# Mixer stage of two fused transformer blocks on one core: conv taps in turns over two channel blocks, four taps instead of eight as matrix products, a reordered projection, and work moved to ScalarE

## The chip, the cores and the metric

One core of one Trainium2 chip runs the whole program. The metric is the device time of one execution in microseconds; the median of several executions is compared.

## What is computed

The reference is a `first_block` and then two layers of a `second_block`, on 256 tokens of width 1024, all in fp32. Only one stage of the first block is touched, the mixer between its two feed-forward layers:

```python
z = _rmsnorm(h, mix_norm[i]) @ w_in[i]
conv_a, conv_gt, q, k, v, r, g_lr = jnp.split(z, SPLIT_POINTS, axis=-1)
y_conv = _conv_module(conv_a, conv_gt, conv_w[i], conv_b[i], conv_ln_g[i], conv_ln_b[i])
y_gla = _gla(q, k, v, r, g_lr, gate_w_up[i], gate_b[i], gla_norm[i])
h = h + jnp.concatenate([y_conv, y_gla], axis=-1) @ w_out[i]
```

`_conv_module` takes `a * sigmoid(b)` (512 channels), runs a causal depthwise convolution of 31 taps over the tokens, adds a bias, and applies a layer norm over the channels and silu. `_gla` is a gated linear attention (here: GLA) of 4 heads over chunks of 64 tokens: `log_sigmoid` of a low-rank gate is summed up within a chunk, its exponentials scale q and k, the scores inside a chunk take one of two products on either side of the diagonal, a state is carried from chunk to chunk, and the result is normalised by head and multiplied by `silu(r)`.

## The kernel before

Every large matrix product is made of three: operands are split into a high part (a cast to fp32r, ScalarE, L208) and a low part (the rest, a subtraction on VectorE, L209), and high x high, low x high and high x low are added up in PSUM. The weights come in one fixed order (`stream_keys`, from `main_keys`, L83) in pieces of 1 MB (SP's DMA queue, L182, three buffers); each piece is split in two halves of 128x1024, tiles `wh` and `wl`, of which eight can be live. `Stream.release` (L222) gives a half back after its last use and at once issues the split of the next one (`pump`, L186). Two shapes of product are used: `chunk` (L667, 24 matmuls of 512 columns for one token tile, L505 to L507) and `chunkT` (L685, 96 matmuls of 256 columns, transposed output, L707).

The order of the instructions of an engine is fixed when the program is built: each takes a priority from its place in the program, and `ahead(-n)` puts it n places further back. The weight splits are put back by 200 (`BEHIND`), the convolution taps by 500 (`CONV_BEHIND`). Side work is written as generators (`spawn`) that are resumed when a count of modelled TensorE time (`tick`) has gone on far enough; `conv_q` is a list of taps from which `tick` takes three for each such microsecond (`CONV_RATE`). At run time an engine executes its instructions in that fixed order and waits where an operand isn't ready.

The mixer (`mixer`, L1062) projects in this order: v of token tile 0 (`val`), the first two channel blocks of the convolution input for both token tiles (`ab`, key `("mi", 0)`), v of tile 1, the low-rank gate `glr`, q and k (`("mi", 2)`), the other two channel blocks (`("mi", 1)`), and r for both tiles (`("mi", 4)`). `glu_T` (L1068) turns the first two blocks so that the channels lie on partitions. The convolution is then, for each of four blocks of 128 channels, a tile `cacc` of 128x256 to which 31 shifted and scaled copies of `glu` are added: the first 23 on VectorE (one tensor_scalar at L832, 22 scalar_tensor_tensor at L839, all reading and writing the same `cacc`), the last 8 on TensorE as products with diagonal matrices (`conv_diag` makes these on ScalarE, L853; `conv_pe`, L856, runs the products at L863 and adds them at L867). `conv_end` (L870) turns `cacc` back to token rows (`cy`), takes the statistics (L876), normalises (`cn`, L884), turns again (`cyT`), applies silu (`cs`, L891) and splits (`cHL`).

GLA runs beside it: `gla_gates` (L899: `z`, `az`, `mz`, `cum`, `epn`, `ee`), `gla_scores` (L943: scaled q and k, `sc`), `gla_state` (L983: `kv`, `S`), `gla_out` (L1015: `o`, the reciprocal root on POOL, `y`, `yT`, `yHL`). The output projection accumulates its attention half (rows of `yHL`) first, for both token tiles, and then its convolution half (rows of `cHL`): 

```python
self.down(0, units(2, 0, self.yg), True, False)
while self.conv_q:
    self.conv_q.pop(0)()
ce = [self.spawn(self.conv_end(t)) for t in range(NT)]
self.down(1, units(2, 1, self.yg), True, False)
for t in range(NT):
    self.need(ce[t])
    self.down(t, units(0, t, self.yc), False, True)
    fin(t)
```

## Time and profile before

| what | us |
|---|---|
| median of three runs | 1488.61 |
| lowest, highest | 1487.82, 1488.87 |
| the profiled execution, its own time | 1489.93 |
| its span | 1488.1 |

The profile is of one execution. A timeline row gives the start, the listed duration, engine, source line, operation, tiles (written <- read), shapes and how many instructions are merged; in brackets the engine's idle time before it and what ended it. Listed durations of neighbouring instructions of one engine overlap a little, so the cost of one in a row of equals is the distance of their starts. A row of the view by stretches gives, for a stretch of time, its length, then the busy time of TensorE's matmuls (PE), weight loads (PEld), VectorE (DVE), ScalarE (ACT) and GpSimd (POOL), the clock granted to TensorE as a share of 2.4 GHz, and the DMA's share and rate.

### The profile page before, as it was taken

To read this page: it belongs to the slowest core of one execution; us is meant where nothing else is said; L and a number is where in the kernel's file an instruction comes from. 1 tells how busy PE (TensorE), PEld (TensorE's weight loads), DVE (VectorE), ACT (ScalarE), POOL (GpSimd) and SP (SyncE) were. 2 spreads that over 40 slices of the span, in tenths; PEclk is the share of its full clock that TensorE was granted. 3 is DMA by queue.
4 is the path that set the end of the run, shared out by engine and by line. 5 is a ranking of instruction groups with operands and counts; after the bars stand their busy time and mean duration, and the time that the engine had idled before them with its cause. 6 is when DMAs were issued, how large, how long until landed. Compare 5 with 4: busy or idle time off the path is not lost.

```text
span 1488.1 us, 23272 instructions
## 1 busy us (share of the span) xinstructions
PE 1459.3 (98%) x9256; PEld 1300.7 (87%) x9256; DVE 1086.9 (73%) x1693; ACT 782.2 (53%) x1238; POOL 55.3 (4%) x60
## 2 busy tenths in 40 slices
PE   8999999999999999999998999999999999999998
PEld 6999989779999879999777899998899988889997
DVE  6876569978875688765678798866988658685554
ACT  6545566265444585444576554446544455554442
POOL 1000000100000000000122100000000000000000
PEclk9999999999999999999999999999999999999999
DMA  8887545138776449786445389863888836376550
GB/s 321 324 310 270 194 147 182 68 131 321 296 298 230 149 156 351 284 317 210 153 144 198 115 331 351 338 236 126 318 345 338 305 140 236 105 296 226 210 201 29
DMA packets 52332, 346.06 MB, mean 233 GB/s; under 512 B 5912, under 2 KB 8704, under 8 KB 11776
## 3 DMA queue, kind: packets, MB, share of 16 engines
q1 hardware_dynamic: 52224, 344.58, 62.4%
q8 instruction: 72, 1.18, 0.3%
q14 instruction: 36, 0.29, 0.1%
HBM read 343.47 MB, written 1.09 MB: 232 GB/s over the span
## 4 chain that ended last, share of the span: by engine, by line
PE 81%; DVE 9%; ACT 4%; issue 2%; DMA 2%; POOL 2%; SPq 0%; POOLq 0%; DVEq 0%; ACTq 0%
PE gu L707 40%; PE acc L506 9%; PE acc L507 9%; PE acc L505 9%; DVE wl L209 4%; PE gu L506 2%; PE gu L507 2%; PE gu L505 2%; DMA raw<-wpack 2%; ACT wh L208 1%; PE xT L586 1%; DVE cacc L839 1%; POOL rn L519 1%; ACT s L1290 1%; PE cv L863 1%
## 5 line engine op out<-in xcount | busy, mean ns | idle before, releaser
L209 DVE TENSOR_TENSOR wl<-raw,wh 128x1024 fp32r<-128x1024 f32 x490 | 588.4, 1221 | 245.1 <-ACT wh L208 241.8
L208 ACT CAST wh<-raw 128x1024 fp32r<-128x1024 f32 x490 | 502.5, 1051 | 389.3 <-DMA raw<-wpack 150.8
L707 PE MATMUL gu<-xh,wh 128*128 128x256 f32 x1728 | 484.1, 280 | 1.1 <-DVE g L751 0.7
L707 PE MATMUL gu<-xl,wh 128*128 128x256 f32 x1728 | 482.5, 279 | 0.0
L707 PE MATMUL gu<-xh,wl 128*128 128x256 f32 x1728 | 482.0, 279 | 0.0
L707 PEld LDWEIGHTS gu<-xh,wh 128*128 128x128 f32 x1728 | 324.7, 188 | 4.4 <-DVE g L751 1.1
L707 PEld LDWEIGHTS gu<-xl,wh 128*128 128x128 f32 x1728 | 324.8, 188 | 2.5
L707 PEld LDWEIGHTS gu<-xh,wl 128*128 128x128 f32 x1728 | 324.8, 188 | 0.0
L506 PE MATMUL acc<-wh,g 128*128 128x512 f32 x528 | 206.7, 391 | 0.0
L507 PE MATMUL acc<-wl,g 128*128 128x512 f32 x528 | 206.0, 390 | 0.0
L505 PE MATMUL acc<-wh,g 128*128 128x512 f32 x528 | 205.8, 391 | 0.0
L462 DVE SCALAR_TENSOR_TENSOR raw<-raw,cact 128x1024 f32<-128x1024 f32 x144 | 171.6, 1218 | 10.0 <-DMA raw<-wpack 10.0
L507 PEld LDWEIGHTS acc<-wl,g 128*128 128x128 f32 x528 | 99.1, 188 | 21.0
L506 PEld LDWEIGHTS acc<-wh,g 128*128 128x128 f32 x528 | 99.1, 188 | 19.8 <-DVE g L514 1.4
L505 PEld LDWEIGHTS acc<-wh,g 128*128 128x128 f32 x528 | 99.1, 188 | 19.2
L749 ACT ACTIVATE s<-gu 128x256 f32<-128x256 f32 x108 | 40.4, 382 | 81.7 <-PE gu L707 81.7
L505 PE MATMUL gu<-wh,xh 128*128 128x512 f32 x192 | 75.7, 395 | 1.8 <-ACT wh L208 1.5
L507 PE MATMUL gu<-wl,xh 128*128 128x512 f32 x192 | 75.1, 393 | 1.5 <-DVE wl L209 1.5
L506 PE MATMUL gu<-wh,xl 128*128 128x512 f32 x192 | 75.3, 393 | 0.5 <-DVE xl L514 0.5
L751 DVE TENSOR_TENSOR g<-gu,s 128x256 f32<-128x256 f32 x108 | 44.4, 420 | 31.4 <-ACT s L749 31.3
L519 POOL TENSOR_TENSOR rn<-nv,neghalf 128x1 f32<-128x1 f32 (+1 forms) x22 | 20.1, 912 | 1238.5 <-DVE nv L533 1020.9
L513 ACT CAST g<-g 128x256 fp32r<-128x256 f32 x108 | 43.1, 405 | 36.1 <-DVE g L751 35.1
(308 smaller groups left out, 1622.1 us busy)
## 6 DMA issues: line engine op xcount, KB each, us to landing
raw<-wpack SPq DMA_DIRECT2D x316, 1024.0 KB, 4.9
gate<-grow SPq DMA_DIRECT2D x6, 512.0 KB, 4.4
row<-rows SPq DMA_DIRECT2D x5, 512.0 KB, 4.8
bias<-fd SPq DMA_DIRECT2D x16, 128.0 KB, 3.9
raw<-wpack SPq DMA_DIRECT2D x2, 512.0 KB, 7.5
out<-h SPq DMA_DIRECT2D x4, 256.0 KB, 2.2
h<-x SPq DMA_DIRECT2D x2, 256.0 KB
h<-x SPq DMA_DIRECT2D x1, 512.0 KB
```

Of the source, the lines that this page charges most:

```text
L208: self.last = k.after(nc.scalar.copy(out=h, in_=raw[:, u, :]))
L209: k.after(nc.vector.tensor_sub(out=l, in0=raw[:, u, :], in1=h.bitcast(F32)))
L462: self.after(nc.vector.scalar_tensor_tensor(out=raw[:, u, :], in0=raw[:, u, :], scalar=1.0, in1=self.cact, op0=ALU.mult, op1=ALU.mult, acc ...
L505: nc.tensor.matmul(out, lhsT=xh, rhs=wh, start=first, stop=False)
L506: nc.tensor.matmul(out, lhsT=xl, rhs=wh, start=False, stop=False)
L507: nc.tensor.matmul(out, lhsT=xh, rhs=wl, start=False, stop=last)
L513: self.nc.scalar.copy(out=dst[0], in_=src),
L519: self.nc.gpsimd.tensor_tensor(out=r, in0=v, in1=self.neghalf[:, :n], op=ALU.pow)
L586: self.last_T = nc.tensor.transpose(ps[:, i, :], xn[hf][:, i * P : (i + 1) * P], self.ident)
L707: nc.tensor.matmul(out, lhsT=ww, rhs=xx, start=first and n == 0, stop=last and n == 2, skip_group_check=True)
L749: nc.scalar.activation(s, b[:, 0, :], AF.Silu)
L751: nc.vector.tensor_mul(out=y, in0=b[:, 1, :], in1=s)
```

## The change

The number of taps done as products falls from 8 to 4. A block's accumulator now starts as the product plus the bias, written by ScalarE, and the remaining 27 taps follow on VectorE, queued alternately for the two blocks of a pair. The pair of blocks 0 and 1 gets its products inside `glu_T`, the pair 2 and 3 right after `glr`; the projection `("mi", 1)` and its weights move ahead of `glr`, q and k. Four pieces of GLA move from VectorE to ScalarE: the minimum in the gates becomes a Relu of the negated sum, four of the eight masked copies of the scores become eight plain copies of 64x64 blocks, the first state is copied there, and the squares of the output are summed there instead of by a reduction.

```diff
--- before.py
+++ after.py
@@ -48,7 +48,7 @@
 
 CONV_RATE = 3.0
 
-CONV_PE = 8
+CONV_PE = 4
 ADA_END = 12.0
 ADA_START = 4
 ADA_STOP = 7
@@ -82,7 +82,7 @@
 
 def main_keys():
     b1 = ffn_keys("f1")
-    b1 += [("mi", c, i) for c in (3, 0, 2, 1, 4) for i in range(2)]
+    b1 += [("mi", c, i) for c in (3, 0, 1, 2, 4) for i in range(2)]
     b1 += [("mo", i) for i in (2, 3, 0, 1)]
     b1 += ffn_keys("f2")
     b1 += [("pp", 0)] + [("pg", i) for i in range(4)]
@@ -824,36 +824,8 @@
         nc.sync.dma_start(out=self.glan, in_=self.row(R_GLA, 512))
         self.diags = self.spawn(self.conv_diag())
 
-    def conv_taps(self, b):
-
-        nc = self.nc
-        cw = COLS["conv_w"][0] + 31 * b
-        acc, glu = self.cacc[:, b, :], self.glu[b]
-        nc.vector.tensor_scalar(
-            out=acc, in0=glu[:, 0:S], scalar1=self.cols[:, cw : cw + 1], scalar2=self.col("conv_b", b),
-            op0=ALU.mult, op1=ALU.add,
-        )
-        for j in range(1, 31 - CONV_PE):
-            def tap(j=j):
-                with self.ahead(-CONV_BEHIND):
-                    nc.vector.scalar_tensor_tensor(
-                        out=acc, in0=glu[:, j : j + S], scalar=self.cols[:, cw + j : cw + j + 1], in1=acc,
-                        op0=ALU.mult, op1=ALU.add,
-                    )
-            self.conv_q.append(tap)
-
-    def conv_diag(self):
-
-        self.diag = {}
-        for b in range(4):
-            self.diag[b] = self.t("row", "diag", [P, 8, P])
-            for n in range(CONV_PE):
-                yield 5.0
-                at = COLS["conv_w"][0] + 31 * b + 31 - CONV_PE + n
-                i = self.nc.scalar.mul(self.diag[b][:, n, :], self.ident, self.cols[:, at : at + 1])
-                self.after(i, self.ws.last)
-
-    def conv_pe(self, bs):
+    def conv(self, bs):
+
 
         nc = self.nc
         ps = self.pst("cv", [P, 2, S])
@@ -864,8 +836,30 @@
                     ps[:, i, :], lhsT=self.diag[b][:, n, :], rhs=self.glu[b][:, j : j + S],
                     start=n == 0, stop=n == CONV_PE - 1,
                 )
-            nc.vector.tensor_add(out=self.cacc[:, b, :], in0=self.cacc[:, b, :], in1=ps[:, i, :])
+            nc.scalar.activation(self.cacc[:, b, :], ps[:, i, :], AF.Identity, bias=self.col("conv_b", b))
         self.tick(0.43 * CONV_PE * len(bs))
+        for j in range(31 - CONV_PE):
+            for b in bs:
+                def tap(j=j, b=b):
+                    at = COLS["conv_w"][0] + 31 * b + j
+                    acc = self.cacc[:, b, :]
+                    with self.ahead(-CONV_BEHIND):
+                        nc.vector.scalar_tensor_tensor(
+                            out=acc, in0=self.glu[b][:, j : j + S], scalar=self.cols[:, at : at + 1], in1=acc,
+                            op0=ALU.mult, op1=ALU.add,
+                        )
+                self.conv_q.append(tap)
+
+    def conv_diag(self):
+
+        self.diag = {}
+        for b in range(4):
+            self.diag[b] = self.t("row", "diag", [P, CONV_PE, P])
+            for n in range(CONV_PE):
+                yield 5.0
+                at = COLS["conv_w"][0] + 31 * b + 31 - CONV_PE + n
+                i = self.nc.scalar.mul(self.diag[b][:, n, :], self.ident, self.cols[:, at : at + 1])
+                self.after(i, self.ws.last)
 
     def conv_end(self, t):
         nc = self.nc
@@ -905,20 +899,23 @@
         nc.gpsimd.memset(rmask.rearrange("p (c t) -> p c t", t=64)[:, :, 0:1], 0.0)
         for hp in range(2):
             nc.tensor.matmul(pz[:, hp, :], lhsT=self.gup[:, hp * P : (hp + 1) * P], rhs=zt, start=True, stop=True)
+
         az = self.t("g2", "az", [P, 2, S])
         mz = self.t("g2", "mz", [P, 2, S])
+        nb = self.tiny("ngb", 2, 1)
+        nc.vector.tensor_scalar_mul(nb, self.col("gate_b"), -1.0)
         for hp in range(2):
-            b = self.col("gate_b", hp)
-            nc.scalar.activation(az[:, hp, :], pz[:, hp, :], AF.Abs, bias=b)
-            nc.vector.tensor_scalar(out=mz[:, hp, :], in0=pz[:, hp, :], scalar1=b, scalar2=0.0, op0=ALU.add, op1=ALU.min)
+            nc.scalar.activation(az[:, hp, :], pz[:, hp, :], AF.Abs, bias=self.col("gate_b", hp))
+            nc.scalar.activation(mz[:, hp, :], pz[:, hp, :], AF.Relu, scale=-1.0, bias=nb[:, hp : hp + 1])
         nc.scalar.activation(az, az, AF.Exp, scale=-1.0)
         nc.scalar.activation(az, az, AF.Ln, bias=1.0)
         yield 4.0
-        nc.vector.tensor_sub(out=mz, in0=mz, in1=az)
+        nc.vector.tensor_add(out=mz, in0=mz, in1=az)
         cum = self.t("g2", "cum", [P, 2, S])
         for hp in range(2):
             nc.vector.tensor_tensor_scan(cum[:, hp, :], rmask, mz[:, hp, :], 0.0, op0=ALU.mult, op1=ALU.add)
-        T = 1.0 / 16.0
+
+        T = -1.0 / 16.0
         be = self.tiny("be", 8, 1)
         nc.vector.tensor_scalar_mul(
             be.rearrange("p (a b) -> p a b", a=2), cum.rearrange("p a (c t) -> p a c t", t=64)[:, :, :, 63], T
@@ -975,9 +972,11 @@
                         nc.tensor.matmul(
                             ps[:, lu, hp, :], lhsT=kk[rows, hp, tok], rhs=qq[rows, hp, tok], start=True, stop=True
                         )
-                for lu, at in enumerate((K_LOW, K_UP)):
-                    m = self.kc[:, at : at + P].bitcast(I32)[:, None, :].to_broadcast([P, 2, P])
-                    nc.vector.copy_predicated(self.sc[t][:, e, :, :], m, ps[:, lu, :, :])
+                for c in range(2):
+                    cc = slice(64 * c, 64 * c + 64)
+                    nc.scalar.copy(out=self.sc[t][cc, e, :, cc], in_=ps[cc, 0, :, cc])
+                m = self.kc[:, K_UP : K_UP + P].bitcast(I32)[:, None, :].to_broadcast([P, 2, P])
+                nc.vector.copy_predicated(self.sc[t][:, e, :, :], m, ps[:, 1, :, :])
             yield 0.6
 
     def gla_state(self, c):
@@ -996,7 +995,7 @@
             self.states = self.t("b4", "S", [P, 4, 2, P])
         s = self.states[:, c]
         if c == 0:
-            nc.vector.tensor_copy(s, ps)
+            nc.scalar.copy(out=s, in_=ps)
         else:
             for hp in range(2):
                 nc.vector.scalar_tensor_tensor(
@@ -1039,9 +1038,9 @@
                         ps[64 * cc : 64 * cc + 64, hp, :], lhsT=self.qp[rows, hp, 64 * c : 64 * c + 64],
                         rhs=self.st[c][rows, hp, :], start=False, stop=True, skip_group_check=True,
                     )
-            sq = self.t("ev", "sq", [P, 2, P])
-            nc.scalar.activation(sq, ps, AF.Square)
-            nc.vector.tensor_reduce(out=ss.rearrange("p (a b) -> p a b", b=2)[:, :, e], in_=sq, op=ALU.add, axis=AX.X)
+            for hp in range(2):
+                h = 2 * hp + e
+                nc.scalar.activation(self.junk()[:, 0:P], ps[:, hp, :], AF.Square, accum_out=ss[:, h : h + 1])
         nc.vector.tensor_scalar(out=ss, in0=ss, scalar1=1.0 / P, scalar2=EPS, op0=ALU.mult, op1=ALU.add)
         r = self.rsqrt(ss, 4, f"g{t}")
         yield 3.5
@@ -1072,9 +1071,9 @@
             if t == NT - 1:
                 for i in range(2):
                     nc.scalar.copy(out=self.glu[i][:, 30 : 30 + S], in_=pt[i])
-                yield 0.5
-                for i in range(2):
-                    self.conv_taps(i)
+                self.conv_rate = CONV_RATE
+                yield 2.0
+                self.conv((0, 1))
 
         def ab(t):
             b = self.psg("ab")
@@ -1092,12 +1091,18 @@
                 self.vt = self.t("b4", "v", [P, NT, 512])
             nc.scalar.copy(out=self.vt[:, t, :], in_=ps)
 
+        self.need(self.diags)
         val(0)
         pt = [self.pst("gluT", [P, S]) for _ in range(2)]
         ab(0)
         ab(1)
-        self.conv_rate = CONV_RATE
         val(1)
+        banks = [self.psa("ab", i, [P, 2, S]) for i in range(2)]
+        self.chunkT(("mi", 1), banks)
+        for i, b in enumerate(banks):
+            sg = self.t("ev", "sig")
+            nc.scalar.activation(sg, b[:, 1, :], AF.Sigmoid)
+            nc.vector.tensor_mul(out=self.glu[2 + i][:, 30 : 30 + S], in0=b[:, 0, :], in1=sg)
 
         pz = self.psg("glr", [P, S])
         for k in range(KT):
@@ -1105,6 +1110,7 @@
                 pz, (self.wglr[0][:, k, :], self.wglr[1][:, k, :]), (self.xh[:, :, k, :], self.xl[:, :, k, :]),
                 k == 0, k == KT - 1,
             )
+        self.conv((2, 3))
         zt = self.t("ev", "glrT", [16, S])
         nc.scalar.copy(out=zt, in_=pz[0:16, :])
 
@@ -1116,15 +1122,6 @@
         banks = [self.psg("qk", [P, 2, S]) for _ in range(2)]
         self.chunkT(("mi", 2), banks)
         scores = self.spawn(self.gla_scores(banks, gates))
-        banks = [self.psa("ab", i, [P, 2, S]) for i in range(2)]
-        self.chunkT(("mi", 1), banks)
-        for i, b in enumerate(banks):
-            sg = self.t("ev", "sig")
-            nc.scalar.activation(sg, b[:, 1, :], AF.Sigmoid)
-            nc.vector.tensor_mul(out=self.glu[2 + i][:, 30 : 30 + S], in0=b[:, 0, :], in1=sg)
-            self.conv_taps(2 + i)
-        self.need(self.diags)
-        self.conv_pe((0, 1))
         states = self.spawn(self.gla_states(scores))
         outs = []
         for t in range(NT):
@@ -1135,7 +1132,6 @@
             nc.scalar.activation(self.rt[:, t, :], ps, AF.Silu)
             nc.gpsimd.tensor_mul(out=self.rt[:, t, :], in0=self.rt[:, t, :], in1=self.glan)
             outs.append(self.spawn(self.gla_out(t, [scores, states])))
-        self.conv_pe((2, 3))
         for o in outs:
             self.need(o)
         self.new_acc()
```

## Rows read from the trace of the kernel before

**Rows 1.** The page: busy time and share of the span of each engine.

```profile
PE 1459.3 (98%) x9256; PEld 1300.7 (87%) x9256; DVE 1086.9 (73%) x1693; ACT 782.2 (53%) x1238; POOL 55.3 (4%) x60
```

**Rows 2.** View by stretches; columns as told above.

```profile
223.70:299.80 76.10, 74.30 (x485) 63.37 (x484) 71.56 (x159) 31.93 (x49) 6.55 (x4) 1.00 0.32 120
```

**Rows 3.** Timeline of VectorE, the end of the convolution.

```profile
294.20 4.64 DVE L839 SCALAR_TENSOR_TENSOR cacc<-glu,cols,cacc 128x256 f32<-128x256 f32 x9
298.95 0.42 DVE L867 TENSOR_TENSOR cacc<-cacc,cv 128x256 f32<-128x256 f32 x1
299.79 1.30 DVE L876 BATCH_NORM_STATS2 cst<-cy 128x6 f32<-128x512 f32 x2 [0.42 <-PE cy L874]
303.47 2.35 DVE L209 TENSOR_TENSOR wl<-raw,wh 128x1024 fp32r<-128x1024 f32 x2
```

**Rows 4.** Timeline of TensorE, a product group and the output projection.

```profile
278.96 3.61 PE L863 MATMUL cv<-glu,diag 128*128 128x256 f32 x16
282.41 0.61 PE L1028 MATMUL o<-v,sc 128*128 128x128 f32 x4
...
301.64 0.39 PE L507 MATMUL acc<-wl,yHL 128*128 128x512 f32 x1
301.87 0.40 PE L505 MATMUL acc<-wh,yHL 128*128 128x512 f32 x1
...
304.57 0.39 PE L507 MATMUL acc<-wl,yHL 128*128 128x512 f32 x1
306.06 0.73 PE L505 MATMUL acc<-wh,cHL 128*128 128x512 f32 x2 [1.10 <-ACT cHL L513]
```

**Rows 5.** Timeline of VectorE, where the taps begin.

```profile
223.75 0.73 DVE L832 TENSOR_SCALAR cacc<-glu,cols 128x256 f32<-128x256 f32 x2
...
224.79 2.35 DVE L209 TENSOR_TENSOR wl<-raw,wh 128x1024 fp32r<-128x1024 f32 x2
227.06 3.25 DVE L839 SCALAR_TENSOR_TENSOR cacc<-glu,cols,cacc 128x256 f32<-128x256 f32 x8
230.25 0.48 DVE L913 TENSOR_SCALAR mz<-z,cols 128x256 f32<-128x256 f32 x1
```

**Rows 6.** Groups of VectorE from 223.7 to 299.7 us: busy, mean ns | idle before.

```profile
L839 DVE SCALAR_TENSOR_TENSOR cacc<-glu,cols,cacc 128x256 f32<-128x256 f32 x88 | 38.2, 488 | 0.3
L209 DVE TENSOR_TENSOR wl<-raw,wh 128x1024 fp32r<-128x1024 f32 x15 | 17.9, 1217 | 0.7 <-ACT wh L208 0.7
L980 DVE COPY_PREDICATED sc<-kc,sc 128x256 f32<-128x256 int32 x8 | 3.0, 431 | 0.0
...
L1044 DVE TENSOR_REDUCE gs<-sq 128x2 f32<-128x256 f32 x4 | 1.6, 412 | 1.0 <-ACT sq L1043 1.0
```

**Rows 7.** Timeline of ScalarE, the copies of glu.

```profile
222.48 0.64 ACT L1074 COPY glu<-gluT 128x256 f32<-128x256 f32 x2
```

**Rows 8.** Chain of waits, one chunkT product: start, length.

```profile
122.24 11.20 PE gu L707 x96
```

**Rows 9.** Timeline of VectorE, weight splits and taps.

```profile
278.09 3.48 DVE L209 TENSOR_TENSOR wl<-raw,wh 128x1024 fp32r<-128x1024 f32 x3
281.50 3.07 DVE L839 SCALAR_TENSOR_TENSOR cacc<-glu,cols,cacc 128x256 f32<-128x256 f32 x5
```

**Rows 10.** By stretches around a wait of TensorE, and TensorE's timeline there.

```profile
814.00:816.00 2.00, 0.68 (x4) 0.24 (x2) 1.90 (x2) 0.59 (x1) 1.82 (x1) 1.00 0.00 0
816.00:818.00 2.00, 1.31 (x6) 1.31 (x7) 0.63 (x1) 0.16 (x1) 0.00 (x0) 0.52 0.00 0
818.00:820.00 2.00, 2.00 (x11) 1.77 (x10) 0.58 (x1) 1.30 (x3) 0.00 (x0) 0.63 0.00 0
...
816.69 1.11 PE L1310 MATMUL aT<-kc,s 128*128 128x128 f32 x4 [2.01 <-DVE on L1347]
```

**Rows 11.** Timelines of ScalarE and VectorE, first and late step of GLA.

```profile
229.74 0.47 ACT L912 ACTIVATE az<-z,cols 128x256 f32<-128x256 f32 x1 [1.76 <-PE z L907]
...
286.40 0.68 DVE L514 TENSOR_TENSOR yHL<-yT,yHL 128x512 fp32r<-128x512 f32 x1
```

## The prediction, made before the change was run

> **What bounds the kernel now.** I read the page first. TensorE is busy for 98% of the span and VectorE for 73% [rows 1]: over the whole kernel TensorE is the bound, but these are averages over stages. The edit lies in one stage, the mixer, so I cut that stage out. From 223.70 to 299.80 us, from the first convolution tap to the layer norm of the convolution, VectorE is busy for 71.56 of 76.10 us, TensorE for 74.30 [rows 2]. Both are nearly full; which one ends the stage shows only in time order. On VectorE the last tap and the last addition end at 299.37 and the statistics of the layer norm start at 299.79 [rows 3]. On TensorE the first half of the output projection (the attention half) lasts until 304.96; then it waits 1.10 us for the split convolution output, the tile cHL, which comes at 306.06 [rows 4]. So two chains end within about 1.1 us of each other, and the later one is VectorE's: taps, then 6.27 us from statistics to cHL (306.06 - 299.79). From there TensorE runs on with what waited for cHL. A change that only shortens TensorE's work here can gain nothing unless VectorE ends sooner too.
>
> **The change, part by part.**
>
> *Products of the convolution.* Sixteen records of a pair of blocks take 3.45 us (278.96 to 282.41) [rows 4], and there are 64 of them. Half of them go: TensorE loses 6.9 us of work. Its own slack is the 1.1 us above, so this comes to about 8 us of slack in front of cHL, not to a gain.
>
> *Taps.* Before, a block has one TENSOR_SCALAR, 22 chained taps, and one addition of the product; after, 27 taps. That is 108 taps for 88. Eight taps that start at 227.06 take until 230.25, 0.40 us each [rows 5]. So +20 x 0.40 = +7.9 us on VectorE. Gone are four TENSOR_SCALARs (0.33 each, the pair from 223.75), 1.3 us, and four additions (0.42 listed [rows 3], of which 0.08 lies under the next instruction, as 2.35 listed for two weight splits [rows 5] against 1.22 for one shows), 1.4 us.
>
> *In turns.* What this part can give is small, because the taps already run in turns where two blocks are at hand: only the last nine, of one block alone, take 4.64 us, 0.52 each [rows 3], against 0.40 [rows 5]. So -9 x 0.12 = -1.1 us. The Trainium skill says otherwise (VectorE: DVE Perf Modes, "The DRAIN you can't avoid"): each instruction waits for the pipe to empty, so that chained and unchained ones take the same time. By that rule the 1.1 us would be missing from the sum; these two rows contradict it.
>
> *To ScalarE.* VectorE loses four of eight copy_predicated (0.43 listed, 0.35 net: 1.4 us), four reductions (0.41 listed, 0.33 net: 1.3 us) with the 1.0 us of waits in front of them [rows 6], two mz (0.48 listed [rows 5], 0.40 net, less about 0.1 for the new negated bias: 0.7 us) and one copy of a state tile (as a copy_predicated, 0.35). Together 4.8 us. ScalarE, busy for 31.93 of 76.10 us [rows 2], takes on some 6 us: four product evacuations, two Relu, eight score copies, a state copy, and eight squares with sums for four without. Its free time hides that; without that cover each copy would hold VectorE's copy_predicated behind it, with the taps behind those, so I allow 0 to 2 us and take 0.
>
> *Sum for VectorE:* 7.9 - 1.3 - 1.4 - 1.1 - 4.8 = -0.7 us. The turn-taking and the relief pay for the taps taken back, no more.
>
> *Late start.* Before, taps start at 223.75, 0.6 us after the copies of glu end (222.48 + 0.64) [rows 7]. After, they need the products (3.45 us, 1.7 for the first block) and ScalarE's evacuation, so about 226.5. VectorE has two weight splits in that time (224.79 to 227.06 [rows 5]); the 1.0 us ahead of them and perhaps 0.4 us behind stay idle. Bounds 0 and 3.5 us; I take +1.4, since the splits cover most. Sum so far: +0.7 us.
>
> *Second conv input ahead of q and k.* The same matmuls and weight splits change places, its own DMAs and the later ones follow in that order on SP's queue, and all are prefetched: no cost by itself. But the gates' chain starts later: by the 96 records of the second conv input, 11.20 us [rows 8], and two product groups, 6.9 us. That is 18.1 us; the cover between q/k and the output projection falls to the r projection alone. TensorE will wait there. It can: it ends early by the 8 us above and what the stall leaves.
>
> *What runs early instead.* This is the term that decides. When the attention half of w_out has been used, its four buffer halves are released and the next layer's weights are cast (ScalarE) and split (VectorE, 1.22 listed [rows 6], 1.14 net). Today that happens after the last tap: the splits stand at 303.47 and later [rows 3]. After, TensorE comes to that point between about 286 us (GLA as short as its instructions allow) and 298 (304.96 - 6.9), ahead of the last tap at some 300. Does a split go ahead of a tap that is ready? In the trace it does: three splits of w_out stand from 278.09, though some of them are not used before 306, and the taps go on behind them at 281.50 [rows 9]. In the program a split is put 200 places behind its release, a tap 500 behind its own place, so the last two dozen taps stand behind. Each split that gets ahead delays the convolution by 1.14 us: 0 to 4.5 us, nothing below since none is taken away. I take three of four, 3.4 us.
>
> *The clock.* TensorE waits in front of cHL for some 8 us with only short transposes. At 814 to 816 us it was busy for 0.68 of 2.00 us, waited 2.01, and the clock granted over the next 2 us was 0.52: its 1.2 GHz level [rows 10]. The next work then runs at half speed until the clock is back; from 818 to 820 it was still 0.63. The work lost there is (1 - 0.52) x 2 + (1 - 0.63) x 2 = 1.7 us. The cost is 0 to 2.2 us (the transposes too); I take +1.7.
>
> *Total:* 0.7 + 3.4 + 1.7 = +5.8 us. The profiled execution took 1489.93 us (span 1488.1), 1.3 us above the median of the three timed runs, 1488.61; the sum is a difference and I put it on the median: 1494.4 us.
>
> **The rivals.** A difference under 0.2%, 3.0 us, can't be told from none here.
>
> *Faster: VectorE ends sooner.* The splits stay behind the taps, TensorE keeps its clock, and the evenly supplied taps fill the waits of VectorE. These are 4.5 us today (76.10 - 71.56 [rows 2]), of which 1.0 is in the sum; if the other 3.5 went and the late start cost nothing, -0.7 - 3.5 = -4.2, 1484.4 us. TensorE's shorter work would allow it down to about -8. For it: taps of two blocks are always at hand. Against it: the order on VectorE is fixed, and an instruction that waits for another engine holds the taps behind it. It decides if all taps end before about 296 us. Chance 0.16.
>
> *No change.* The splits do not get ahead, or one does, and the clock dips at most briefly: +0.7 to +2.4 and 1489 to 1491 us. This is also the case in which the change does nothing of what its words say: turns that were there already, products that were not the bound. Chance 0.28.
>
> *Later attention half.* From the first Abs of the gates at 229.74 to the first split yHL at 286.40 it is 56.7 us [rows 11]. Were it as long again, started 18.1 us later, yHL would come at 304.5, and the attention half (10.9 us: 48 matmuls at 0.23 us, 301.64 to 301.87 [rows 4]) would end at 315.4, 9.3 us past 306.06: 1498 us. It decides only if the chain takes over 47 us. Against it: most of those 56.7 us it waited for other work in front of it. Chance 0.08.
>
> **How the numbers follow.** The forecast itself, slower by 3 to 10 us, has 0.48; together with the last rival slower is 0.56, no change 0.28, faster 0.16. The range leaves out the faster rival, 0.16, and a little at the top: from 1486.0 (VectorE 2.6 us better, no splits, no clock) to 1499.5 (late start 3.5, four splits, clock 2.2, and one more us of waits for ScalarE, 10.9 in all).
>
> **What would show it.** Right: 108 taps at 0.40 us to the end, 32 conv records, VectorE again full until 300 us or later; TensorE idle for several us ahead of cHL, with a granted clock below 1 there; splits for the next layer between taps; cHL at about 310 instead of 306 on the same scale. Wrong: VectorE with gaps ahead of the layer norm, or the last tap before 297 us, would leave the gain to TensorE; splits behind the last tap would take 3.4 us from the sum; a full clock through the wait 1.7; and an attention half that ends after the taps would make the GLA chain the bound.

## The result: slower by 14.0 us, and the profile after

The changed kernel takes 1502.78 us (median of 4 runs, 1502.30 to 1503.02) against 1488.74 for the kernel before (4 runs): ratio 1.0094, interval 1.0076 to 1.0111. The forecast was 1494.4 with a range up to 1499.5: the sign was right, the size was not. The profiled execution took 1502.79 us, its span is 1501.0, 12.9 more than before.

First the page of the kernel after, busy time and share of each engine (as [rows 1]):

```profile
PE 1460.3 (97%) x9224; PEld 1300.8 (87%) x9224; DVE 1089.9 (73%) x1695; ACT 781.5 (52%) x1248; POOL 53.8 (4%) x60
```

Then its view by stretches, from the first tap to the layer norm (as [rows 2]):

```profile
224.15:310.49 86.34, 74.53 (x460) 62.44 (x459) 77.14 (x162) 39.27 (x77) 5.11 (x4) 0.90 0.31 117
```

Over the whole kernel almost nothing moved; in the stage, 76.10 us became 86.34. VectorE is busy for 77.14 instead of 71.56, and idle for 9.20 instead of 4.54. TensorE's granted clock, 1.00 before, is 0.90.

To see where the 12.9 us arise, I cut the span at marks from the timelines, two of which were not shown before. First the kernel before (VectorE's first normalised tile of the mixer, TensorE's first matmul of the next layer), then the kernel after (the same two, and TensorE's first cHL):

```profile
206.20 0.48 DVE L575 TENSOR_SCALAR xn<-h,rn 128x512 f32<-128x512 f32 x1 [0.45 <-POOL rn L519]
318.76 0.50 PE L505 MATMUL gu<-wh,xh 128*128 128x512 f32 x1 [0.36 <-ACT xh L513]
```

```profile
204.79 0.49 DVE L575 TENSOR_SCALAR xn<-h,rn 128x512 f32<-128x512 f32 x1 [0.44 <-POOL rn L519]
317.21 1.22 PE L505 MATMUL acc<-wh,cHL 128*128 128x512 f32 x2 [1.60 <-ACT cHL L513]
331.32 0.49 PE L505 MATMUL gu<-wh,xh 128*128 128x512 f32 x1 [0.35 <-ACT xh L513]
```

| part of the span | before | after | more |
|---|---|---|---|
| up to the mixer's first tile | 206.20 | 204.79 | -1.41 |
| to the first tap | 17.50 | 19.36 | +1.86 |
| taps, to the layer norm | 76.10 | 86.34 | +10.24 |
| layer norm to cHL | 6.26 | 6.72 | +0.46 |
| cHL to the next layer | 12.70 | 14.11 | +1.41 |
| rest | 1169.34 | 1169.68 | +0.34 |

Groups of VectorE from 224.2 to 310.4 us (as [rows 6]), and then, with the total, how often and the longest, what it waited for from 219.9 to 311:

```profile
L847 DVE SCALAR_TENSOR_TENSOR cacc<-glu,cols,cacc 128x256 f32<-128x256 f32 x108 | 45.8, 488 | 0.4 <-ACT cacc L839 0.2
L209 DVE TENSOR_TENSOR wl<-raw,wh 128x1024 fp32r<-128x1024 f32 x17 | 20.4, 1218 | 1.9 <-ACT wh L208 1.9
...
L1044 DVE TENSOR_SCALAR gs<-gs 128x4 f32<-128x4 f32 x2 | 1.4, 696 | 0.0
```

```profile
DVE sc L979 <- ACT sc L977: 3.5, 1, 3.5
DVE wl L209 <- ACT wh L208: 2.3, 4, 1.4
DVE y L1048 <- POOL rg L519: 1.5, 2, 0.9
DVE yHL L514 <- ACT yHL L513: 1.0, 1, 1.0
```

In the kernel before only 14 splits begin in the stage, against 17 here: the 15 of [rows 6] count one that began ahead of the first tap and ended at 223.83 (first line below). And in the kernel after one split more stands ahead of the first tap (second line):

```profile
221.37 2.46 DVE L209 TENSOR_TENSOR wl<-raw,wh 128x1024 fp32r<-128x1024 f32 x2
```

```profile
222.81 1.22 DVE L209 TENSOR_TENSOR wl<-raw,wh 128x1024 fp32r<-128x1024 f32 x1 [0.38 <-ACT wh L208]
```

The timeline of VectorE goes on from there:

```profile
224.20 3.90 DVE L847 SCALAR_TENSOR_TENSOR cacc<-glu,cols,cacc 128x256 f32<-128x256 f32 x8 [0.17 <-ACT cacc L839]
...
285.11 1.23 DVE L1044 TENSOR_SCALAR gs<-gs 128x4 f32<-128x4 f32 x1
...
293.13 9.19 DVE L847 SCALAR_TENSOR_TENSOR cacc<-glu,cols,cacc 128x256 f32<-128x256 f32 x23
302.51 4.63 DVE L209 TENSOR_TENSOR wl<-raw,wh 128x1024 fp32r<-128x1024 f32 x4 [0.19 <-ACT wh L208]
307.06 2.85 DVE L847 SCALAR_TENSOR_TENSOR cacc<-glu,cols,cacc 128x256 f32<-128x256 f32 x7
310.48 1.29 DVE L870 BATCH_NORM_STATS2 cst<-cy 128x6 f32<-128x512 f32 x2 [0.57 <-PE cy L868]
```

Four weight splits of the next layer stand ahead of the last seven taps. And TensorE has nothing to do at the end. Its timeline follows (keT and yT are tiles that it turns for GLA, as it turns cy and cyT for the convolution), then its clock by stretches:

```profile
259.80 0.69 PE L963 MATMUL keT<-kc,ke 128*128 128x128 f32 x2 [2.56 <-DVE ke L950]
...
288.13 1.23 PE L1055 MATMUL yT<-kc,y 128*128 128x128 f32 x4 [2.80 <-DVE y L1048]
...
303.27 0.39 PE L507 MATMUL acc<-wl,yHL 128*128 128x512 f32 x1
309.57 1.30 PE L868 MATMUL cy<-kc,cacc 128*128 128x128 f32 x4 [5.92 <-DVE cacc L847]
313.67 1.94 PE L882 MATMUL cyT<-kc,cn 128*128 128x128 f32 x8 [2.80 <-DVE cn L878]
```

```profile
259.80:266.50 6.70, 6.70 (x19) 5.04 (x20) 6.16 (x15) 1.01 (x2) 0.00 (x0) 0.52 0.34 108
266.50:287.00 20.50, 18.83 (x131) 13.94 (x129) 15.71 (x29) 12.39 (x34) 3.50 (x3) 0.99 0.22 75
287.00:293.80 6.80, 5.17 (x16) 3.80 (x17) 4.59 (x14) 1.17 (x2) 1.61 (x2) 0.52 0.32 135
293.80:307.50 13.70, 9.85 (x46) 7.79 (x44) 13.51 (x28) 3.89 (x4) 0.00 (x0) 0.99 0.10 31
307.50:321.10 13.60, 7.13 (x22) 5.28 (x23) 7.02 (x17) 4.04 (x10) 1.08 (x2) 0.51 0.35 143
```

Three times the clock stands near 0.5 (1.2 GHz), each time about an idle stretch of TensorE: 2.56 us ahead of keT, 2.80 ahead of yT, 5.92 and 2.80 ahead of cy and cyT. The first two lie within GLA.

### The profile page after: what moved, and what is told of

Same layout as the page of the kernel before. It is cut to its first block, busy times and chain, and to the rows that moved or that the text cites. A ratio compares the mean times of both kernels' runs of the same rounds, so it can differ in the third digit from the quotient of the medians.

```text
span 1501.0 us, 23228 instructions
## 1 busy us (share of the span) xinstructions
PE 1460.3 (97%) x9224; PEld 1300.8 (87%) x9224; DVE 1089.9 (73%) x1695; ACT 781.5 (52%) x1248; POOL 53.8 (4%) x60
## 4 chain that ended last, share of the span: by engine, by line
PE 85%; DVE 7%; ACT 4%; issue 2%; POOL 2%; DMA 0%; POOLq 0%; DVEq 0%; ACTq 0%
PE gu L707 40%; PE acc L506 9%; PE acc L505 9%; PE acc L507 9%; DVE wl L209 3%; PE gu L506 2%; PE gu L507 2%; PE gu L505 2%; PE xT L586 1%; POOL rn L519 1%; ACT wh L208 1%; PE qk L707 1%; PE ab L707 1%; ACT s L1286 1%; ACT junk L524 1%
```

## Experiments

Theory 1: VectorE ends the stage, by more taps, by early splits and by waits that hold its queue. Theory 2: GLA, which starts later by the new order, ends it. Medians of before beside these runs were 1488.8 to 1489.7 us.

**Fewer products, in either structure.** `CONV_PE` set back to 8 in the kernel after, and to 4 in the kernel before:

```diff
-CONV_PE = 4
+CONV_PE = 8
```

> The changed kernel with eight taps as products again, all else as changed. Theory 1 (VectorE ends the stage: its work and its waits set the end): 16 taps fewer are 16 x 0.40 = 6.3 us less on VectorE, and the 6.9 us more on TensorE fall into its waits: 1502.8 - 6.3 = 1496.5 us, 1495 if the clock dips less. Theory 2 (the loss is the GLA chain that lost its cover by the new order; the number of taps hardly matters): within 2 us of 1502.8. Rival (TensorE is the bound after all): 1509.

1495.99 us (1493.11 to 1497.55), ratio 1.0040 (1.0027 to 1.0052).

> The kernel before with four products for eight, nothing else: 16 more taps on VectorE, 6.9 us less on TensorE. Theory 1: VectorE ends 6.3 us later, some splits get ahead of taps, so 1488.7 + 6 to + 10 us: 1495 to 1499. Rival (TensorE is the bound of the stage): up to 6.9 us faster, 1482.

1511.39 us (1511.10 to 1515.03), ratio 1.0151 (1.0131 to 1.0170). Going from 8 to 4 products costs 22 us in the old structure and 6.8 in the new one. The old one pays twice, as VectorE's timeline of before_4_products shows:

```profile
294.65 4.63 DVE L209 TENSOR_TENSOR wl<-raw,wh 128x1024 fp32r<-128x1024 f32 x4 [0.45 <-ACT wh L208]
299.20 7.29 DVE L839 SCALAR_TENSOR_TENSOR cacc<-glu,cols,cacc 128x256 f32<-128x256 f32 x16
...
310.50 0.42 DVE L867 TENSOR_TENSOR cacc<-cacc,cv 128x256 f32<-128x256 f32 x1 [3.55 <-PE cv L863]
310.95 5.69 DVE L839 SCALAR_TENSOR_TENSOR cacc<-glu,cols,cacc 128x256 f32<-128x256 f32 x11
```

The same four splits are early, a product is late, and the last 11 taps are one chain alone, 0.52 us each.

With 8 products the kernel after fails in another way: VectorE's last tap is done, and it waits for TensorE, whose attention half is late.

```profile
306.12 1.30 DVE L870 BATCH_NORM_STATS2 cst<-cy 128x6 f32<-128x512 f32 x2 [4.62 <-PE cy L868]
```

**The order.** q and k again ahead of the second conv input, first with 4 products, then with 8:

```diff
-    b1 += [("mi", c, i) for c in (3, 0, 1, 2, 4) for i in range(2)]
+    b1 += [("mi", c, i) for c in (3, 0, 2, 1, 4) for i in range(2)]
...
-        banks = [self.psa("ab", i, [P, 2, S]) for i in range(2)]
-        self.chunkT(("mi", 1), banks)
...
-        self.conv((2, 3))
...
         scores = self.spawn(self.gla_scores(banks, gates))
+        banks = [self.psa("ab", i, [P, 2, S]) for i in range(2)]
+        self.chunkT(("mi", 1), banks)
...
+        self.conv((2, 3))
```

> The changed kernel with q and k projected ahead of the second conv input again, that pair's products right after its input; four products, turns and the work on ScalarE stay. Theory 1 (work on VectorE, 20 taps more): the work is the same, so within 3 us of 1502.8. Theory 2 (lost cover: about 5 us of VectorE's waits behind the GLA chain and TensorE's low clock from 260 to 267 us come from the order): 1502.8 - 5 to - 8, so 1495 to 1498 us, and the wait of the masked score copy on the copies by ScalarE (3.5 us) is gone.

1502.46 us (1500.85 to 1505.00): no difference in time. But the waits are not the same. The clock from 258 to 268 us is 1.00 here, the score copies wait for nothing, and VectorE idles for 8.3 us of the stage all the same, in other places, the longest ahead of a weight split. Its first score copy, that split and the statistics:

```profile
259.62 0.44 DVE L979 COPY_PREDICATED sc<-kc,sc 128x256 f32<-128x256 int32 x1
...
275.33 1.23 DVE L209 TENSOR_TENSOR wl<-raw,wh 128x1024 fp32r<-128x1024 f32 x1 [2.10 <-ACT wh L208]
...
308.20 1.30 DVE L870 BATCH_NORM_STATS2 cst<-cy 128x6 f32<-128x512 f32 x2 [0.57 <-PE cy L868]
```

So Theory 2 fails at 4 products, and a kernel can be as slow without the wait of 3.5 us that is the largest in the kernel after.

> The kernel after with 8 products again and with q and k ahead of the second conv input again; what is left of the change is the taps in turns and the work given to ScalarE. Theory 1 (VectorE ends the stage: taps, early splits, waits): 16 taps of 0.41 us (6.6) and four early splits (4) leave VectorE against the same order with 4 products, which wrote the conv's statistics at 308.4: some 298, a little ahead of the kernel before; TensorE's attention half ends at about 303 as there, so 1486 to 1490. Theory 2 (what made 1496.0 with 8 products was the GLA that came late by the new order): with the old order it is not late, 1486 to 1490 as well. Against both: if the work on ScalarE is what holds TensorE's GLA up, the time stays at 1494 to 1497.

1499.96 us (1498.40 to 1500.19), ratio 1.0063 (1.0048 to 1.0078): both theories missed, and so did "the order made GLA late" as the reason for 1495.99. At 8 products the new order is 4.0 us the better one. VectorE of the kernel with 1499.96 waits for ScalarE's copy of the products at the start of each pair of blocks:

```profile
DVE cacc L847 <- ACT cacc L839: 4.2, 2, 2.3
```

**The relief alone, and without it.** The four ScalarE moves (Relu for mz, the lower score copies, the state copy, squares with sums, as in the change's diff) put into the kernel before; and taken out of the kernel after.

> The kernel before with the four moves of work to ScalarE alone (z's minimum, the lower score copies, the state's copy, the sums of squares): 8 products, taps chain by chain and the old order stay. If VectorE alone ends the stage, up to 4.8 us fewer: 1484 to 1486. If the copies on ScalarE come back as waits of TensorE and VectorE, as the waits of 3.5 and 1.4 us in the kernel after suggest, or TensorE's attention half is the bound within a microsecond or two: 1487 to 1491.

1489.36 us (1488.09 to 1491.35), ratio 0.9996 (0.9987 to 1.0006): no gain. VectorE is free sooner and waits for TensorE (its last wait, of 0.42 us before [rows 3]):

```profile
DVE cst L876 <- PE cy L874: 2.5, 1, 2.5
```

> The kernel after with its four moves of work to ScalarE undone. Theory 1 (VectorE ends the stage and every microsecond on it counts): VectorE gets 4.8 us of work back, 1507 to 1508. Rival (the relief is given back as waits behind ScalarE's copies, the 3.5 us ahead of the first score copy and the 1.4 us ahead of a split): 1502 to 1504.

1505.46 us (1503.61 to 1508.39): 2.7 more than after, between the two expectations. The relief counts here, at 2.7 us instead of 4.8. And the wait ahead of the score copies stays, without any copy on ScalarE:

```profile
DVE sc L976 <- PE sc L971: 2.5, 2, 2.0
```

So most of the 3.5 us named "ACT sc" in the kernel after is TensorE's, and ScalarE only came last. In the kernel after ScalarE waits for TensorE's scores itself and begins its copies 0.56 us before VectorE goes on at 269.47:

```profile
268.91 1.09 ACT L977 COPY sc<-sc 64x128 f32<-64x128 f32 x4 [0.49 <-PE sc L972]
```

**Turns with the old chain.** The kernel before with the moves, two blocks' taps queued alternately, TENSOR_SCALAR first and the 8 products added at the end, as before:

```diff
-            self.conv_q.append(tap)
+            out.append(tap)
...
+        if b % 2 == 0:
+            self.conv_even = pair
+        else:
+            for two in zip(self.conv_even, pair):
+                self.conv_q.extend(two)
```

> The kernel before with the ScalarE moves and with its taps in turns, but each chain still begins with VectorE's TENSOR_SCALAR and its 8 products are still added at the end. If the 10 us that the changed conv costs in the old order with 8 products (1500.0 against 1489.4) come from the products that VectorE's first taps have to wait for: 1488 to 1490. If they come from the turns themselves (a pair starts late, both chains end together): 1494 to 1500.

1489.59 us (1487.92 to 1491.14), ratio 1.0003. The kernel with 1499.96 differs from it in the place of the products, ahead of the taps and not behind them, and in what goes with it (ScalarE's copy for VectorE's first operation and addition, the place where taps begin to be queued). So at 8 products it is putting them first, with what goes with it, that costs 10.4 us; turns cost nothing.

**The early splits.**

> The changed kernel, with the weight splits that the attention half of the output projection releases held back until the convolution is normalised. Theory 1: four splits of 1.14 us leave the path in front of the last taps: 1502.8 - 4.5 = 1498.3 us. Rival (the last taps are not on the path, or the splits come back as a wait at the start of the next layer): within 1 us of 1502.8.

1502.49 us (1500.97 to 1504.51), inconclusive. The edit was

```diff
         ce = [self.spawn(self.conv_end(t)) for t in range(NT)]
+        self.held = True
...
+            if t == 0:
+                self.hold(False)
             self.down(t, units(0, t, self.yc), False, True)
```

and it left the order as it was: four splits still stood ahead of the last seven taps. The next one moves them, by a larger distance in the planner's places:

```diff
-            with k.ahead(-BEHIND):
+            with k.ahead(-k.behind):
...
+        self.behind = 900
         self.down(1, units(2, 1, self.yg), True, False)
```

> The kernel after, with the four early splits of f1's second group put behind the last taps on VectorE's queue. Theory 1: VectorE ends the stage, so cst comes sooner by what stands ahead of it, 4.0 to 4.6 us, and the cHL matmuls with it; part comes back where the splits now stand among the statistics: 1498 to 1499.5. Rival: the splits only trade places with a wait of VectorE's further on (for TensorE's cy, or for f1's transposes), and the time stays at 1502 to 1503.

1500.54 us (1499.51 to 1502.06): 2.2 less. One split stands behind the last tap, two among the statistics:

```profile
303.54 1.23 DVE L209 TENSOR_TENSOR wl<-raw,wh 128x1024 fp32r<-128x1024 f32 x1
304.68 1.29 DVE L871 BATCH_NORM_STATS2 cst<-cy 128x6 f32<-128x512 f32 x2
...
305.97 1.20 DVE L209 TENSOR_TENSOR wl<-raw,wh 128x1024 fp32r<-128x1024 f32 x1
```

The statistics start 5.8 us sooner (310.48 to 304.68; 1.3 of it is a shorter wait ahead of the score copies, see below), and in its span of 1500.2 only 0.8 us is left of that. The splits now lengthen the way from there to cHL by 2.0 us (313.37 - 304.68 against 6.72), the way from cHL to the next layer takes 0.8 more, and the rest of the kernel 2.3 more: that layer's TensorE waits 1.8 us for VectorE where it waited 0.3.

**The clock.** Matmuls of no use, whose results nothing reads, in TensorE's idle stretches.

```diff
         self.down(1, units(2, 1, self.yg), True, False)
+        wm = self.psg("wm")
+        for _ in range(30):
+            nc.tensor.matmul(wm, lhsT=self.ones_r, rhs=self.xh[:, 0, 0:4, :], start=True, stop=True)
```

> The kernel after, with 30 matmuls of no use behind the attention half, which TensorE runs in its idle stretch ahead of cy. They hold nothing up unless they last longer than the idle 5.9 us. If the low clock behind the stretch costs what its rows show, 48 cHL matmuls at 0.43 instead of 0.23 us until about 321, some 4 us less 1 to 2 that the normalisation takes anyway: 1499 to 1501. If the clock falls all the same, in the 2.8 and 1.6 us of idle time behind cy and cyT, 1502 to 1503.

1500.13 us (1499.24 to 1501.43). 13 of the 30 ran ahead of and between the yT transposes, and the clock stayed at 1.00 there; 17 ran ahead of cy, and behind them it fell all the same. But this run shows something more. Ahead of keT, where nothing was added, TensorE idles as in the kernel after, and here the clock held. By stretches, from 258 to 268 us, the kernel after and then after_warm_matmuls:

```profile
258.00:268.00 10.00, 8.20 (x26) 6.05 (x26) 7.96 (x20) 2.81 (x10) 0.00 (x0) 0.66 0.44 160
```

```profile
258.00:268.00 10.00, 7.46 (x42) 5.70 (x42) 9.32 (x22) 4.97 (x17) 0.00 (x0) 1.00 0.49 189
```

And VectorE's timeline a little later, in the kernel after, after_splits_held, after_splits_behind and after_warm_matmuls:

```profile
269.47 1.00 DVE L979 COPY_PREDICATED sc<-kc,sc 128x256 f32<-128x256 int32 x2 [3.51 <-ACT sc L977]
```

```profile
269.03 1.00 DVE L979 COPY_PREDICATED sc<-kc,sc 128x256 f32<-128x256 int32 x2 [2.19 <-ACT sc L977]
```

```profile
268.01 1.00 DVE L980 COPY_PREDICATED sc<-kc,sc 128x256 f32<-128x256 int32 x2 [2.18 <-ACT sc L978]
```

```profile
267.27 1.00 DVE L979 COPY_PREDICATED sc<-kc,sc 128x256 f32<-128x256 int32 x2 [0.57 <-ACT sc L977]
```

Up to there these four kernels run the same instructions in the same order, and each idles 2.55 or 2.56 us ahead of keT. The granted clock from 258 to 268 us was 0.66, 0.83, 0.83 and 1.00, the wait 3.51, 2.19, 2.18 and 0.57 us. On TensorE's queue the r matmuls stand between the first and the second half of the scores. In the kernel after they follow each other at 0.43 us until the clock is back and at 0.23 from then on, and so the second half of the scores comes late:

```profile
262.59 0.63 PE L505 MATMUL r<-wh,xh 128*128 128x512 f32 x1
...
267.94 0.49 PE L972 MATMUL sc<-qp,kn 64*128 64x128 f32 x2
```

VectorE's score copy waits for them, and the taps behind it.

Then on purpose: matmuls ahead of the first keT, yT, cy and cyT (18 of 256 columns, 10, 22 and 10 of 512), written where the transposes then write:

```diff
+            if t == 0:
+                for _ in range(18):
+                    nc.tensor.matmul(pt, lhsT=self.ones_r, rhs=self.xh[:, 0, 0:2, :], start=True, stop=True)
             for hp in range(2):
                 nc.tensor.transpose(pt[:, hp, :], ket[:, hp, tok], self.ident)
```

> The kernel after with matmuls of no use ahead of each of the four things that TensorE idles for: 18 of 256 columns ahead of the first keT, 10 of 512 ahead of the first yT, 22 ahead of the first cy, 10 ahead of the first cyT. If the low clock behind these idle stretches makes part of the 14 us (the first score copy waits 3.5 us for ScalarE, 0.6 where TensorE kept its clock; the cHL matmuls take 13.35 instead of 11.95): 2.9 and 1.4 less, and up to 1 in the attention half: 1497 to 1499. If VectorE's own work alone sets the end, or the matmuls come in the way: 1501 to 1503.

1496.22 us (1495.19 to 1497.85), ratio 1.0050 (1.0036 to 1.0063): 6.6 of the 14.0 us are back, more than expected. But the added matmuls also changed VectorE's order: 13 splits stand in the stage instead of 17, and the last 30 taps have none among them. The score copies wait 0.5 us, and at the end VectorE waits 2.33 us for TensorE's cy. So I took the places apart, ahead of keT alone, then keT, yT and cyT, with the splits left early.

> The kernel after with 18 matmuls of no use ahead of the first keT alone; the four early splits stay ahead of the last taps. If the low clock behind that idle stretch makes the wait of 3.5 us ahead of the first score copy, that wait shrinks to 0.5 and the time with it: 1499.5 to 1500.5. If VectorE's later waits take it up: 1501.5 to 1503.

1501.83 us (1500.75 to 1503.02). The wait is gone as expected (3.51 to 0.51) and the statistics come at 307.73 instead of 310.48, but only 1.0 us of it reaches the median, with ranges that overlap, and 2.0 the profiled span. TensorE still idles at the end, and from 310 to 320 us its clock is 0.54:

```profile
306.82 1.30 PE L868 MATMUL cy<-kc,cacc 128*128 128x128 f32 x4 [5.13 <-DVE cacc L847]
310.92 1.94 PE L882 MATMUL cyT<-kc,cn 128*128 128x128 f32 x8 [2.80 <-DVE cn L878]
```

> The kernel after with the matmuls of no use ahead of the first keT, the first yT and the first cyT, not ahead of cy; the four early splits stay ahead of the last taps. Against after_kept_busy (1496.2) it has the splits back and TensorE idle ahead of cy. If clock and splits share the 6.6 us that after_kept_busy got back, with 4.5 for the splits: 3 to 4 us less than after, 1498.5 to 1500. If the clock alone made it: 1496 to 1497.

1505.46 us (1499.56 to 1507.00), a miss: the matmuls ahead of cyT write into its bank, waited for VectorE as cyT does, and then ran for 4.6 us at half clock on the path:

```profile
312.26 4.60 PE L883 MATMUL cyT<-xh,ones_r 128*128 128x512 f32 x10 [2.80 <-DVE cn L878]
```

So the share of the clock can't be read off as one number. What after_kept_busy got back came with both: no early splits and no low clock at the end.

**A version that beats both?** In the kernel before the relief of VectorE gains nothing, so I moved one product's work from TensorE to VectorE: the kernel before with the moves and 7 products, chain by chain and in turns.

> The kernel before with the ScalarE moves and 7 products instead of 8. VectorE gets 4 taps of 0.41 us more (1.6), of the 3.4 us that it only waits now; TensorE loses 8 products of 0.23 us (1.8). If TensorE ends the stage once VectorE is relieved: 1487.5 to 1488.5. If VectorE still ends it: 1489.5 to 1491. An early split more that falls ahead of the last taps adds 1.2.

1488.85 us (1486.47 to 1491.41), ratio 0.9998 (0.9990 to 1.0007): the same time. In its profile the clock from 290 to 300 us is 0.91.

> The kernel before with the ScalarE moves, its taps in turns and 7 products. With 8 products VectorE waits 4.2 us for the last product and 10.4 in all, so TensorE ends the stage; 8 products of 0.23 us fewer bring TensorE's end forward by 1.8, and 4 taps of 0.41 us go into VectorE's waits: 1487.5 to 1488.5. If TensorE's clock falls in one of its idle stretches, as in the kernel with 7 products chain by chain (0.91 from 280 to 300), or VectorE becomes the bound: 1489 to 1490.5.

1495.42 us (1492.77 to 1497.17), ratio 1.0046 (1.0033 to 1.0060), a miss. All taps end early, but two splits moved in between the statistics, TensorE idled 3.36 us ahead of cyT, and the clock from 300 to 310 us was 0.72. I found nothing that beats the kernel before.

## Why the prediction was right in its sign and wrong in its size

*Bound.* Right. VectorE ended the stage, TensorE idled ahead of cy, cyT and cHL for 5.92, 2.80 and 1.60 us, and its lost products bought nothing: its attention half ended at 303.66 (303.27 + 0.39), not between 286 and 298.

*VectorE's own work.* Forecast -0.7 us, of which 1.0 were waits, so +0.3 busy. Measured: 77.14 - 71.56 = 5.58 busy, less three more splits in the stage (14 to 17, 3 x 1.14 = 3.4), so +2.2. Two pieces make the difference. Taps less turns were put at 7.9 - 1.1 = 6.8; the groups list 45.8 against 38.2 [rows 6], 7.6. And a TENSOR_SCALAR of 128x4 took 1.23 us at 285.11 and 0.16 the second time (1.4 for the two), which adds 1.1 us. The relief was sized right as work: net of overlaps the copies, reductions, mz and the state copy are 1.1 + 1.5 + 0.8 + 0.4 = 3.8 us less in the trace, as forecast (4.8 less the waits). In time it is worth 2.7 us by the run without it.

*Late start.* The stretch to the first tap grew by 1.86 us, and the forecast was +1.4 of idle time. But 1.1 us of it is one split that had stood behind the first operation of the chains [rows 5]; VectorE's idle time there grew from 4.63 to 5.03, 0.4 us. At 4 products this cost little.

*Early splits.* Right in kind, four instead of three: 4.6 us, 1.1 of which only pays for the split that moved ahead of the first tap. Moving them gave 2.2 us of the time, so an early split is only partly a loss: put behind the taps, it came in the way of the layer norm and of the next layer.

*Clock at the end.* Forecast 1.7; the two parts behind the layer norm took 0.46 + 1.41 = 1.9 more.

*Two sums.* 20 x 0.40 is 8.0, not 7.9. And the terms named for the top of the range come to 10.5 (3.5 + 4.5 + 2.2 + 1.0 - 0.7), not 10.9. Neither changes the account.

*The step that failed:* "its free time hides that ... I allow 0 to 2 us and take 0", and beside it "TensorE will wait there. It can." With the 1.0 us taken off, I had VectorE's idle time shrink from 4.54 to 3.5; it grew to 9.20, 5.7 us of the 7.1 that the sum of 5.8 lacks against the 12.9 of the spans. The waits were not the moved copies' own: without the four moves VectorE idles for 8.6 us. The largest piece in the profile is 3.5 us, of which about 0.5 is ScalarE's copy and 3.0 is TensorE's. TensorE's idle stretch ahead of GLA, which I named and called free, was followed there by the low clock, the r matmuls took nearly twice as long, and the second half of the scores came late to a VectorE queue in which the taps stand behind. I priced the clock only at the place where TensorE waits last.

How far that wait accounts for the time is another matter. Taken away by itself it gave back 1.0 us, and with the old order it is gone and the time is the same. In every kernel here with 4 products and no added matmuls VectorE idles for 7.0 to 10.5 us of the stage, whatever the order (after 9.2, without the moves 8.6, old order 8.3, before_4_products 10.5). So it is shown that VectorE waits more there, not less; why the waits come back elsewhere when one is taken away stays open.

*Rivals.* "Later attention half" (1498) is what the kernel after becomes at 8 products, where VectorE waits 4.62 us for cy; at 4 products it did not decide, nor did the order. "Faster" failed at the point named for it: the last tap ended at 309.9, not before 296.

*In turns, by the Trainium skill.* The prediction took from it (VectorE: DVE Perf Modes, "The DRAIN you can't avoid") that chained taps are as fast as taps in turns. That section does say that the next instruction does not start until the pipe is empty. But it adds that one that is not held starts earlier, and what it timed is instructions with and without a semaphore after each, not a chain against turns. The runs again show a difference: 11 taps of one chain took 5.69 us, 0.52 each, in before_4_products; 23 in turns took 9.19, 0.40 each, in the kernel after.

*Left open.* The runs form a ladder from the kernel before to the kernel after: the moves 1489.36, with turns 1489.59, with the products first 1499.96, with the new order 1495.99, with 4 products 1502.78. So at 8 products putting them first costs 10.4 us and the order gives 4.0 back, and 4 products then cost 6.8. (The kernel before, timed beside each, moved by up to 1 us.) The shares depend on the path: with the old order, 4 products for 8 cost 2.5 us and the new order nothing. What the products first cost at 4 was not tried by itself. How the 14.0 us divide between splits and clock is open too: they change together whenever the order does.

## What to carry to other kernels

An idle stretch of an engine that "has time" is free only if nothing in order behind it feeds the bound: price the clock and the lateness at every idle stretch that a change opens, not only at the last. When the bound is an in-order queue, list what waits in it, and ask of each whether its producer gets slower. A wait that stands large in a profile is still not a price: take it away by itself and see what comes back (3.0 us here, of which 1.0 did). And when two engines end a stage within a microsecond, relief of one alone gains nothing: the four moves were worth 0 us before the change and 2.7 after it.

## Not expected of the hardware

The same 2.55 to 2.56 us of idle time on TensorE, in the same order of instructions, was followed by a clock of 1.00 in one execution and by 0.83 or 0.66 (over 10 us) in others. Seventeen added matmuls, with 1.94 us of idle time between them and cy, did not keep the clock either: from 304 to 314 us it was 0.64 in after_warm_matmuls. And the TENSOR_SCALAR of four columns that took 1.23 us (285.11 to 286.34 in the kernel after) ended with a multiplication on GpSimd, 284.76 to 286.31, in GpSimd's timeline:

```profile
284.76 1.55 POOL L1133 TENSOR_TENSOR r<-r,glan 128x512 f32<-128x512 f32 x1 [8.93 <-ACT r L1132]
```

In the kernel before, with no such multiplication beside it, the same operation took 0.16. It is no single case, and not only in the kernel after. In the kernel before a tap that met the same multiplication (280.55 to 282.70) took 1.49 us where the others take 0.48, and in the kernel after a tap beside the first multiplication (274.46 to 275.83) took 1.52. Where VectorE was at work when the multiplication began, the multiplication took longer instead (2.37 us at 271.93 in the kernel before, 1.37 at 274.46 in the kernel after). The tap of the kernel before:

```profile
281.50 1.49 DVE L839 SCALAR_TENSOR_TENSOR cacc<-glu,cols,cacc 128x256 f32<-128x256 f32 x1
```

The Trainium skill (SBUF — State Buffer, "SBUF: two separate sides") says that VectorE, in some of its operations, and GpSimd take a shared pair of ports under an exclusive lock for a whole instruction, and the other one blocks; these rows agree. That the one slows the other was not tried by itself.
